# Sums of a long convolution's spectral products: the second set on VectorE instead of GpSimd

## Chip, cores and metric

One core of a Trainium2 chip runs the whole program. The metric is the device time of one execution in microseconds (us), taken as the median of several runs. The profile is one further execution, recorded by the hardware profiler.

## What is computed

A hybrid encoder layer over 512 positions and 1024 channels, batch 1, in fp32: a token mixer of three branches (long convolution, 2-D neighbourhood attention, short gated convolution), then cross-attention into 256 memory tokens, then a gated MLP. The change lies in the first branch:

```python
def long_conv(z, kf, bias):
    L = z.shape[1]
    zf32 = z.astype(jnp.float32)
    zf = jnp.fft.rfft(zf32, n=2 * L, axis=1)
    y = jnp.fft.irfft(zf * kf[None], n=2 * L, axis=1)[:, :L]
    return (y + zf32 * bias.astype(jnp.float32)).astype(z.dtype)

def hyena_mixer(u, short_w, kf, bias):
    u = dwconv3(u, short_w)
    v, x1, x2 = jnp.split(u, 3, axis=-1)
    z = x1 * long_conv(v, kf[:, 0], bias[0])
    return x2 * long_conv(z, kf[:, 1], bias[1])
```

So two convolutions of 512 channels follow each other, each gated by a projected column.

## The kernel before

Every fp32 product is made of three TensorE passes (`mm3`, lines 88 to 90) over operands that are split in a high part (`high`, L75, on ScalarE) and a low part (`low`, L78, on VectorE unless another engine is named). Weights come as 128x1024 blocks (`wr`, loaded on SyncE's queue at L110 into three buffers) and are split into `wh` and `wl`.

The long convolution runs in the loop over `parts` in `go` (two convolutions by two halves of 256 channels), four rounds that are called round 0 to 3 here. In round n the program

- makes the forward sums (`conv_forward`): PE multiplies the folded, transposed input (`sh`, `sl`) with cosine and sine waves (`wavefh`, `wavefl`, tiles `aux`), ScalarE and VectorE turn them into `fly` tiles (L523 to L529), and VectorE multiplies these by the filter's spectrum `kst` into two tiles `ab` of 128x2048 (L533 to L537): `a` and `b`, 1290 and 1291 in round 0, 1477 and 1478 in round 1;
- sums each of the two in four instructions (L543 to L546, 128x512 each, in place), the set of `a` on VectorE and the set of `b` on GpSimd;
- turns the previous round's products back (`conv_back`: PE with `waveeh`, `waveoh`; VectorE gates the result in place in `vx`, L570);
- prepares the next round's input (`conv_in`): PE transposes two `vx` tiles (L490, four instructions for each), ScalarE makes `sh`, VectorE makes `sl`;
- splits the sums for the next turn back (`conv_split`: `ych` and `ysh` on ScalarE, `ycl` and `ysl` on VectorE).

Beside these, `beside` feeds three projections per round (24 matmuls of 128x512 each, tiles `mm`) and pieces of the short convolution (`scg`, `scx`, `sct`, `yc`; L580, L323, L331, L585). A tile framework builds the program: it puts each engine's instructions in an order of its own, from the order in which the code asks for them and from its own costs, so a change of one engine moves others. On the chip each engine works through its list in that order.

GpSimd has little else here: it adds the third tap of eight projected columns (L329) and makes the low parts of some constants before, and adds attention masks (L686) later.

Of the kernel before, what the change touches and what calls it, by code (L numbers as in the profile page):

```python
# [9 lines left out]
ALU = mybir.AluOpType  # L10
# [35 lines left out]
def shaped(ap, offset, *dims):  # L46

    return bass.AP(ap.tensor, ap.offset + offset, [list(ap.ap[0])] + [list(q) for q in dims])


class Trunk:
# [444 lines left out]
    def conv_forward(self, pool, c, o, folded):  # L496


        nc, v = self.nc, self.nc.vector
        sh, sl = folded  # L500
        k = pool.tile([P, 8, 256], F32, tag="kst", bufs=1, name="kst")
        for i in range(2):
            nc.sync.dma_start(out=k[:, 4 * i : 4 * i + 4], in_=self.kd[o, c, :, 4 * i : 4 * i + 4])
        wh, wl = self.waves["f"]

        def sums(r):

            ps = self.aux_bank()
            for cs in range(2):
                w = slice((2 * r + cs) * P, (2 * r + cs + 1) * P)  # L510
                self.mm3(ps[:, cs * 256 : (cs + 1) * 256], (wh[:, w], wl[:, w]), (sh[:, r, :], sl[:, r, :]), cs == 0, cs == 1)
            return ps

        even, odd, plus = (pool.tile([P, 1024], F32, tag="fly" + q, bufs=1, name="fly") for q in "eop")
        for out, r in ((even, 0), (odd, 1)):
            low, high = out[:, 0:512], out[:, 512:1024]
            far = sums(r + 2)
            self.high(low, far[:])
            near = sums(r)
            if r:  # L520

                high = shaped(out[:], 768, [-256, 2], [1, 256])
                v.tensor_tensor(out=high, in0=near[:].rearrange("p (a b) -> p a b", a=2), in1=low.rearrange("p (a b) -> p a b", a=2),  # L523
                                op=ALU.subtract)
            else:
                v.tensor_tensor(out=high, in0=near[:], in1=low, op=ALU.subtract)
            v.tensor_tensor(out=low, in0=near[:], in1=low, op=ALU.add)
        v.tensor_tensor(out=plus[:], in0=even[:], in1=odd[:], op=ALU.add)
        v.tensor_tensor(out=even[:], in0=even[:], in1=odd[:], op=ALU.subtract)  # L529
        minus = even  # L530
        a, b = (pool.tile([P, 2048], F32, tag="ab", bufs=2, name="ab") for _ in range(2))
        kf = k[:].rearrange("p a b -> p (a b)")
        v.tensor_tensor(out=a[:, 0:1024], in0=plus[:], in1=kf[:, 0:1024], op=ALU.mult)  # L533
        v.tensor_tensor(out=a[:, 1024:2048], in0=minus[:], in1=kf[:, 1024:2048], op=ALU.mult)
        v.tensor_tensor(out=shaped(b[:], 0, [512, 2], [256, 2], [1, 256]), in0=shaped(plus[:], 0, [512, 2], [256, 2], [1, 256]),
                        in1=shaped(kf, 256, [1536, 2], [-256, 2], [1, 256]), op=ALU.mult)
        v.tensor_tensor(out=shaped(b[:], 1024, [256, 4], [1, 256]), in0=shaped(minus[:], 0, [256, 4], [1, 256]),  # L537
                        in1=shaped(kf, 1280, [-256, 4], [1, 256]), op=ALU.mult)
        for t, op, eng in ((a, ALU.add, v), (b, ALU.subtract, nc.gpsimd)):
            def part(i, step):  # L540
                return shaped(t[:], 256 * i, [256 * step, 2], [1, 256])

            eng.tensor_tensor(out=part(0, 4), in0=part(0, 4), in1=part(1, 4), op=op)  # L543
            eng.tensor_tensor(out=part(6, -4), in0=part(6, -4), in1=part(3, 4), op=op)
            eng.tensor_tensor(out=part(1, 2), in0=part(0, 6), in1=part(4, -2), op=ALU.add)
            eng.tensor_tensor(out=part(5, 2), in0=part(0, 6), in1=part(4, -2), op=ALU.subtract)  # L546
        return a, b

    def conv_split(self, pool, y):
# [798 lines left out]
```

## Time and profile before

| | |
|---|---|
| median of 3 runs | 1112.19 us (1111.86 to 1113.84) |
| the profiled execution, its own time | 1114.05 us |
| span of its instructions | 1112.3 us |
| PE busy | 1081.6 us (97% of the span) |
| VectorE (DVE) busy | 696.5 us (63%) |
| ScalarE (ACT) busy | 477.3 us (43%) |
| GpSimd (POOL) busy | 95.4 us (9%) |
| mean granted TensorE clock | 0.99 of full speed |

The span runs from the first instruction to the last, and the execution's own time holds 1.75 us more around it. An engine's busy share is a mean over stages with different limits, so a change in one stage is read from that stage. Times in the rows count from the start of the span; an instruction's line gives its start, its duration, and in brackets how long its engine sat idle before it and what ended the wait.

### The profile page before, as it was taken

How to read it: one execution, taken by the hardware profiler on the slowest of the kernel's cores; microseconds unless marked ns; L12 is line 12 of the kernel's file. 1: busy time of each engine (PE TensorE's matmuls, PEld its weight loads, DVE VectorE, ACT ScalarE, POOL GpSimd, SP SyncE). 2: the span in 40 equal slices, each digit the busy share in tenths (PEclk: the TensorE clock that was granted, in tenths of full speed). 3: DMA queues.
4: the chain of work that ended last, by engine and by line, in shares of the span. 5: the costliest groups of instructions: out<-in, count | busy, mean ns of one | idle time of the engine just before them, and what ended most of it. 6: DMA issues, size and time to landing. Idle time of an engine off the chain costs nothing.

```text
span 1112.3 us, 13562 instructions
## 1 busy us (share of the span) xinstructions
PE 1081.6 (97%) x5232; PEld 903.2 (81%) x5232; DVE 696.5 (63%) x1021; ACT 477.3 (43%) x744; POOL 95.4 (9%) x72
## 2 busy tenths in 40 slices
PE   8889989999999999999999999999999999999997
PEld 6668878887888888888789888889888888888886
DVE  6898799985656564344796546576656565642324
ACT  6553532224557453232565444454444444431221
POOL 0161242221121110000000000000000000000000
PEclk9899999999999999999999999999999999999999
DMA  6354723317423312224526421222222222222212
GB/s 218 105 190 161 246 94 107 103 58 167 125 87 100 112 57 95 95 95 160 200 76 205 156 76 57 76 95 95 95 95 95 95 95 97 102 98 101 95 57 75
DMA packets 43532, 125.48 MB, mean 113 GB/s; under 512 B 5097, under 2 KB 11561, under 8 KB 43468
## 3 DMA queue, kind: packets, MB, share of 16 engines
q1 hardware_dynamic: 43468, 124.62, 33.4%
q8 instruction: 41, 0.67, 0.2%
q14 instruction: 23, 0.19, 0.1%
HBM read 115.16 MB, written 7.34 MB: 110 GB/s over the span
## 4 chain that ended last, share of the span: by engine, by line
PE 82%; DVE 9%; DMA 3%; ACT 2%; issue 2%; POOL 1%; SPq 0%; DVEq 0%; ACTq 0%; POOLq 0%
PE mm L88 25%; PE mm L89 25%; PE mm L90 25%; DVE wl L78 2%; PE aux L725 1%; PE aux L89 1%; PE aux L90 1%; PE aux L88 1%; DMA wr<-in_w_in 1%; PE aux L714 1%; ACT wh L75 1%; PE aux L904 1%; DMA raw<-in_hy_o 1%; POOL w L398 0%; DMA wr<-in_w_out 0%
## 5 line engine op out<-in xcount | busy, mean ns | idle before, releaser
L78 DVE TENSOR_TENSOR wl<-wr,wh 128x1024 fp32r<-128x1024 f32 (+1 forms) x171 | 219.8, 1289 | 254.4 <-ACT wh L75 253.6
L75 ACT ACTIVATE wh<-wr 128x1024 fp32r<-128x1024 f32 (+1 forms) x171 | 180.1, 1054 | 308.1 <-PE mm L89 186.7
L89 PE MATMUL mm<-hl,wh 128*128 128x512 f32 (+1 forms) x448 | 167.5, 374 | 0.0
L88 PE MATMUL mm<-hh,wh 128*128 128x512 f32 (+1 forms) x448 | 167.2, 374 | 0.3 <-ACT hh L75 0.3
L90 PE MATMUL mm<-hh,wl 128*128 128x512 f32 (+1 forms) x448 | 167.4, 374 | 0.0
L88 PE MATMUL mm<-xh,wh 128*128 128x512 f32 x416 | 164.6, 396 | 0.0
L89 PE MATMUL mm<-xl,wh 128*128 128x512 f32 x416 | 163.7, 393 | 0.0
L90 PE MATMUL mm<-xh,wl 128*128 128x512 f32 x416 | 163.6, 393 | 0.0
L89 PEld LDWEIGHTS mm<-hl,wh 128*128 128x128 f32 x448 | 84.4, 188 | 15.0 <-DVE hl L78 0.2
L90 PEld LDWEIGHTS mm<-hh,wl 128*128 128x128 f32 x448 | 84.3, 188 | 15.0
L88 PEld LDWEIGHTS mm<-hh,wh 128*128 128x128 f32 x448 | 84.1, 188 | 15.2 <-ACT hh L75 0.5
L90 PEld LDWEIGHTS mm<-xh,wl 128*128 128x128 f32 x416 | 78.9, 190 | 17.1 <-issue 0.3
L88 PEld LDWEIGHTS mm<-xh,wh 128*128 128x128 f32 x416 | 79.0, 190 | 15.8
L89 PEld LDWEIGHTS mm<-xl,wh 128*128 128x128 f32 x416 | 78.9, 190 | 15.7
L88 PE MATMUL mm<-wh,act 128*128 128x512 f32 x176 | 68.5, 389 | 0.0
L89 PE MATMUL mm<-wl,act 128*128 128x512 f32 x176 | 68.5, 389 | 0.0
L90 PE MATMUL mm<-wh,act 128*128 128x512 f32 x176 | 68.3, 389 | 0.0
L88 PEld LDWEIGHTS mm<-wh,act 128*128 128x128 f32 x176 | 33.0, 188 | 7.1 <-issue 0.3
L75 ACT ACTIVATE act<-u 128x512 fp32r<-128x512 f32 x22 | 13.9, 630 | 57.8 <-DVE u L1024 57.8
L90 PEld LDWEIGHTS mm<-wh,act 128*128 128x128 f32 x176 | 33.0, 188 | 6.9
L89 PEld LDWEIGHTS mm<-wl,act 128*128 128x128 f32 x176 | 33.0, 188 | 6.8
L331 DVE SCALAR_TENSOR_TENSOR u<-mm,cols,u 128x511 f32<-128x511 f32 x44 | 33.0, 751 | 1.5
(342 smaller groups left out, 1938.4 us busy)
## 6 DMA issues: line engine op xcount, KB each, us to landing
wr<-in_w_in SPq DMA_DIRECT2D x55, 512.0 KB, 3.6
wr<-in_ffn_up SPq DMA_DIRECT2D x44, 512.0 KB, 3.5
wr<-in_ffn_down SPq DMA_DIRECT2D x22, 512.0 KB, 3.4
wr<-in_w_branch SPq DMA_DIRECT2D x12, 512.0 KB, 3.4
kd<-kt SPq DMA_DIRECT2D x16, 256.0 KB, 3.9
kst<-kd SPq DMA_DIRECT2D x8, 512.0 KB, 4.9
wr<-in_w_out SPq DMA_DIRECT2D x8, 512.0 KB, 4.3
wr<-in_xa_wk SPq DMA_DIRECT2D x8, 512.0 KB, 3.4
```

Of the source, the lines that this page charges most:

```text
L75: self.nc.scalar.activation(out=out, in_=in_, func=ACT.Copy, bias=0.0, scale=scale)
L78: (eng or self.nc.vector).tensor_tensor(out=out, in0=in_, in1=f(high), op=ALU.subtract)
L88: mm(out, ah, bh, start=first, stop=False)
L89: mm(out, ah, bl, start=False, stop=False)
L90: mm(out, al, bh, start=False, stop=last)
L331: nc.vector.scalar_tensor_tensor(out=out[:, 0 : L - 1], in0=ps[:, 1:L], scalar=self.colvec(w2), in1=out[:, 0 : L - 1], op0=ALU.mult, op1=A ...
L714: nc.tensor.transpose(tr[:, i * P : (i + 1) * P], s[:, i // 2, (i % 2) * P : (i % 2 + 1) * P], self.ident[:])
L725: self.nc.tensor.matmul(po[64 * e : 64 * e + 64, b * P : (b + 1) * P], v[b, j][:, h * 64 : (h + 1) * 64], pt[:, (2 * i + j) * P : (2 * i + ...
L904: self.nc.tensor.transpose(tr[:, k * P : (k + 1) * P], t[:, c : c + P], self.ident[:])
```

## The change

The second set of sums, those of `b`, goes to VectorE, like the first set. No instruction is added or dropped: 16 instructions of 128x512 (four in each of four rounds) leave GpSimd and join VectorE.

```diff
-        for t, op, eng in ((a, ALU.add, v), (b, ALU.subtract, nc.gpsimd)):
+        for t, op in ((a, ALU.add), (b, ALU.subtract)):
             def part(i, step):
                 return shaped(t[:], 256 * i, [256 * step, 2], [1, 256])
 
-            eng.tensor_tensor(out=part(0, 4), in0=part(0, 4), in1=part(1, 4), op=op)
-            eng.tensor_tensor(out=part(6, -4), in0=part(6, -4), in1=part(3, 4), op=op)
-            eng.tensor_tensor(out=part(1, 2), in0=part(0, 6), in1=part(4, -2), op=ALU.add)
-            eng.tensor_tensor(out=part(5, 2), in0=part(0, 6), in1=part(4, -2), op=ALU.subtract)
+            v.tensor_tensor(out=part(0, 4), in0=part(0, 4), in1=part(1, 4), op=op)
+            v.tensor_tensor(out=part(6, -4), in0=part(6, -4), in1=part(3, 4), op=op)
+            v.tensor_tensor(out=part(1, 2), in0=part(0, 6), in1=part(4, -2), op=ALU.add)
+            v.tensor_tensor(out=part(5, 2), in0=part(0, 6), in1=part(4, -2), op=ALU.subtract)
```

The framework then orders the four rounds anew. On VectorE, from round 0's first sum on, before (the numbers tell buffers apart; `vx_1335` is a projected column, `wl_1400` the low part of a weight block):

```order
L543 TENSOR_TENSOR ab_1290<-ab_1290 128x2x256
L544 TENSOR_TENSOR ab_1290<-ab_1290 128x2x256
L323 SCALAR_TENSOR_TENSOR vx_1335<-mm_1310,cols_176,vx_1335 128x511
L545 TENSOR_TENSOR ab_1290<-ab_1290 128x2x256
L546 TENSOR_TENSOR ab_1290<-ab_1290 128x2x256
L78 TENSOR_TENSOR wl_1400<-wr_1401,wh_1399 128x1024
L78 TENSOR_TENSOR sl_1375<-aux_1376,sh_1374 128x4x128
L78 TENSOR_TENSOR sl_1375<-aux_1383,sh_1374 128x4x128
```

On the same engine, from the same place on, with the change:

```order
L543 TENSOR_TENSOR ab_1290<-ab_1290 128x2x256
L544 TENSOR_TENSOR ab_1290<-ab_1290 128x2x256
L543 TENSOR_TENSOR ab_1291<-ab_1291 128x2x256
L545 TENSOR_TENSOR ab_1290<-ab_1290 128x2x256
L546 TENSOR_TENSOR ab_1290<-ab_1290 128x2x256
L544 TENSOR_TENSOR ab_1291<-ab_1291 128x2x256
L323 SCALAR_TENSOR_TENSOR vx_1335<-mm_1310,cols_176,vx_1335 128x511
L545 TENSOR_TENSOR ab_1291<-ab_1291 128x2x256
L546 TENSOR_TENSOR ab_1291<-ab_1291 128x2x256
L78 TENSOR_TENSOR sl_1375<-aux_1376,sh_1374 128x4x128
L78 TENSOR_TENSOR sl_1375<-aux_1383,sh_1374 128x4x128
```

The second set stands among the first, and the low part of the weight block has gone behind both `sl` (and behind `ycl` and `ysl`). In the same way `wl_1578`, which stood ahead of round 1's sums, now stands behind them. ScalarE's two `sh` of round 0 now stand ahead of the copy `tap` of `vx_1335`, which waits for the L323 above.

On PE, the transposes of round 1 stood in front of the projection `mm_1640`; this piece of the difference shows where they stand now:

```order
 L90 MATMUL mm_1583<-xh_427,wl_1400 128x512
-L490 MATMUL aux_1611<-ident_178,vx_455 128x128 x4
-L490 MATMUL aux_1618<-ident_178,vx_459 128x128 x4
 L88 MATMUL mm_1640<-xh_379,wh_1492 128x512
 L89 MATMUL mm_1640<-xl_380,wh_1492 128x512
 L90 MATMUL mm_1640<-xh_379,wl_1493 128x512
 L88 MATMUL mm_1640<-xh_385,wh_1492 128x512
+L490 MATMUL aux_1611<-ident_178,vx_455 128x128 x4
 L89 MATMUL mm_1640<-xl_386,wh_1492 128x512
 L90 MATMUL mm_1640<-xh_385,wl_1493 128x512
```

The first four come four matmuls later, the second four twelve; in round 2 it is one matmul and eight.

On SyncE's queue, loads of weights and of the spectrum of rounds 2 and 3, before:

```order
L110 DMA wr_1729<-in_w_in 128x1024
L110 DMA wr_1814<-in_w_in 128x1024
L503 DMA kst_1670<-kd_611 128x1024 x2
L110 DMA wr_1871<-in_w_in 128x1024
L110 DMA wr_1964<-in_w_in 128x1024
L110 DMA wr_2049<-in_w_in 128x1024
L503 DMA kst_1905<-kd_611 128x1024 x2
```

With the change:

```order
L110 DMA wr_1729<-in_w_in 128x1024
L503 DMA kst_1670<-kd_611 128x1024 x2
L110 DMA wr_1814<-in_w_in 128x1024
L110 DMA wr_1871<-in_w_in 128x1024
L110 DMA wr_1964<-in_w_in 128x1024
L503 DMA kst_1905<-kd_611 128x1024 x2
L110 DMA wr_2049<-in_w_in 128x1024
```

`wr_1814` and `wr_2049` have each gone behind the two loads of a round's spectrum. `wr_1814` takes the buffer of the block that `wl_1578` reads.

## Rows read from the trace of the kernel before

**Rows 1.** Windows: length, busy time of each engine (instructions), granted clock, DMA share, GB/s.

```profile
140.00:262.00 122.00, 115.51 (x632) 100.30 (x632) 110.67 (x119) 39.66 (x53) 30.98 (x19) 0.99 0.28 92
...
161.60:165.20 3.60, 3.60 (x17) 3.36 (x16) 3.60 (x5) 1.20 (x2) 0.00 (x0) 0.53 0.03 10
...
216.20:226.00 9.80, 8.30 (x48) 7.32 (x48) 9.24 (x13) 2.63 (x4) 0.00 (x0) 1.00 0.48 161
...
274.30:277.90 3.60, 3.60 (x10) 2.80 (x9) 3.60 (x6) 1.74 (x5) 2.00 (x2) 0.53 0.66 218
```

**Rows 2.** Timeline of PE: its waits in the four rounds, and the next one after.

```profile
160.10 0.38 PE L89 MATMUL aux<-sl,wavefh 128*128 128x256 f32 x1 [3.57 <-DVE sl L78]
...
182.90 0.75 PE L490 MATMUL aux<-ident,vx 128*128 128x128 f32 x4 [1.06 <-DVE vx L570]
...
209.32 1.34 PE L490 MATMUL aux<-ident,vx 128*128 128x128 f32 x8 [0.36 <-DVE vx L570]
...
215.76 0.39 PE L90 MATMUL mm<-xh,wl 128*128 128x512 f32 x1
215.99 0.28 PE L88 MATMUL aux<-sh,wavefh 128*128 128x256 f32 x1
217.76 0.38 PE L89 MATMUL aux<-sl,wavefh 128*128 128x256 f32 x1 [1.50 <-DVE sl L78]
...
272.84 0.36 PE L695 MATMUL aux<-kb,qa 128*128 128x256 f32 x1 [1.93 <-DMA kb<-ka]
```

**Rows 3.** Timeline of VectorE: round 0's sums, then three places of rounds 1 and 2.

```profile
150.85 0.68 DVE L543 TENSOR_TENSOR ab<-ab 128x512 f32<-128x512 f32 x1
151.46 1.78 DVE L544 TENSOR_TENSOR ab<-ab 128x512 f32<-128x512 f32 x1
153.16 0.74 DVE L323 SCALAR_TENSOR_TENSOR vx<-mm,cols,vx 128x511 f32<-128x511 f32 x1
153.82 1.11 DVE L545 TENSOR_TENSOR ab<-ab 128x512 f32<-128x512 f32 x1
154.86 1.78 DVE L546 TENSOR_TENSOR ab<-ab 128x512 f32<-128x512 f32 x1
156.56 2.29 DVE L78 TENSOR_TENSOR wl<-wr,wh 128x1024 fp32r<-128x1024 f32 x1
158.77 1.27 DVE L78 TENSOR_TENSOR sl<-aux,sh 128x512 fp32r<-128x512 f32 x2
...
176.46 0.68 DVE L543 TENSOR_TENSOR ab<-ab 128x512 f32<-128x512 f32 x1
...
184.50 1.22 DVE L78 TENSOR_TENSOR ysl<-ab,ysh 128x1024 fp32r<-128x1024 f32 x1 [1.66 <-ACT ysh L75]
...
202.88 0.68 DVE L543 TENSOR_TENSOR ab<-ab 128x512 f32<-128x512 f32 x1
```

**Rows 4.** Timeline of GpSimd in round 0.

```profile
152.65 1.73 POOL L544 TENSOR_TENSOR ab<-ab 128x512 f32<-128x512 f32 x1
154.46 1.62 POOL L545 TENSOR_TENSOR ab<-ab 128x512 f32<-128x512 f32 x1
156.04 1.72 POOL L546 TENSOR_TENSOR ab<-ab 128x512 f32<-128x512 f32 x1
```

**Rows 5.** Timelines of VectorE and GpSimd around 33.5 us, in another stage.

```profile
33.43 0.16 DVE L153 TENSOR_TENSOR rstdq<-rstdq,rstdm 128x4 f32<-128x4 f32 x1
33.62 1.18 DVE L154 TENSOR_SCALAR rstdq<-rstdq 128x4 f32<-128x4 f32 x1
...
33.49 2.52 POOL L398 TENSOR_TENSOR w<-wr 128x512 f32<-128x512 f32 x2 [33.05 <-DMA wr<-in_hy_w]
```

**Rows 6.** Timeline of ScalarE: high parts in rounds 0 and 1.

```profile
154.57 1.08 ACT L75 ACTIVATE sh<-aux 128x512 fp32r<-128x512 f32 x2
...
183.41 1.06 ACT L75 ACTIVATE ysh<-ab 128x1024 fp32r<-128x1024 f32 x1 [12.40 <-POOL ab L546]
```

**Rows 7.** DMA issues: tile, queue, count, KB each, median us from issue to landing.

```profile
wr<-in_w_in SPq DMA_DIRECT2D x55, 512.0 KB, 3.6
```

## The prediction

> **What bounds the kernel now.** I read the windows of the four rounds first. From 140 to 262 us PE works 115.51 of 122 us and VectorE 110.67 [rows 1]: PE is the bound, but VectorE is nearly as full, and the 6.49 us that PE idles there can only come from engines that feed it. PE's timeline names these waits: 3.57, 1.06, 0.36 and 1.50 us [rows 2], 6.49 together, each ended by VectorE: by `sl`, the input of the next round's sums, or by L570, the gated column that PE transposes. After the longest one PE's clock fell: from 161.6 to 165.2 us the granted clock was 0.53 of full speed, near its lower level of 1.2 GHz [rows 1], so these 3.60 us did the work of 0.53 x 3.6 = 1.9, a loss of 1.7. So 6.5 + 1.7 = 8.2 us is the most that a faster VectorE can give in this stage.
>
> Then VectorE's timeline, to see why it is late. Four instructions of one size, 128x512, all in SBUF, last 0.68, 1.78, 1.11 and 1.78 us [rows 3]. GpSimd's timeline explains the long ones: its adds end at 154.38, 156.08 and 157.76 [rows 4], and VectorE's L545, L546 and the split `wl` behind them end at 154.93, 156.64 and 158.85 [rows 3], 0.55, 0.56 and 1.09 us after these ends, which is about what each takes by itself from start to start. They had been issued earlier and were held until GpSimd's add was done. That the hold doesn't go by size is seen elsewhere: on 128x4 elements VectorE takes 0.16 us, and 1.18 us for the next one, just when GpSimd starts an add [rows 5]. Instructions that read PSUM (L323, L570, `sl`) keep their short times.
>
> **The change part by part.** *The sums.* Unheld, an add costs 0.61 us from start to start (150.85 to 151.46); held, 1.70 (154.86 to 156.56) [rows 3]. These are the two ends for each of the 32 adds that VectorE now makes. I take 0.61, since nothing of GpSimd's runs beside them but one L329 in round 0. Before, a round's set cost VectorE 156.56 - 150.85 - 0.66 (L323, 153.16 to 153.82) = 5.05 us [rows 3]; now both sets cost 8 x 0.61 = 4.88. So 16 adds come to VectorE and its list becomes 0.17 us shorter per round. GpSimd's chain ends with the set; ScalarE's `ysh`, which waited 12.40 us for it in round 1 [rows 6], follows VectorE instead.
>
> By the Trainium skill, "VectorE: DVE Perf Modes", section on the TRN2 errata, an fp32 add of N elements takes (N+151)/0.96 ns, 0.69 us for 512; that speaks against the change. If starts were so far apart, both sets would take 5.5 us, and a round would grow by 0.5 us, an estimate. The trace's duration of 0.68 agrees, but the starts lie 0.61 apart [rows 3], and these count in a full list.
>
> *Round 0.* From 150.85: eight adds 4.88, L323 0.66, so `sl` begins at 156.39 and ends 1.27 later at 157.66, because the held `wl` no longer stands ahead of it; `sh` was done at 155.65 even behind the wait that it now precedes [rows 6]. PE starts there instead of at 160.10: **2.4 us**. It then has waited 1.2 us instead of 3.57.
>
> *The clock.* After waits of 1.06 and 1.50 us PE kept full speed (1.00 around the latter), after 1.93 it fell to 0.53 for 3.6 us [rows 1, 2]. A wait of 1.2 lies with the former, so I count the whole **1.7 us**; the ends are 0 and 1.7.
>
> *Round 1.* VectorE's adds began 25.61 us after those of round 0 (176.46 - 150.85) [rows 3]. Now: less 0.17, less 1.1 (the hold on `wl`), less 1.1 (`wl_1578`, moved behind the adds): 23.2, so they start at 174.1. The first L570 is seventh and ends at 174.1 + 6 x 0.61 + 0.68 = 178.4, the second at 180.3. PE was ready for the second transposes at 181.84 (1.06 before 182.90); now 4.1 earlier, plus twelve matmuls of 0.23 (215.76 to 215.99), at 180.5: no wait. For the first it is ready eight matmuls and four transposes (0.75) before, at 177.9: 0.5 of wait [rows 2]. Of 1.06, **0.5 us** is gained.
>
> *Round 2.* Between the adds of rounds 1 and 2 lay 26.42 us (202.88 - 176.46); less 0.17 and less the idle 1.66 in front of `ysl` that `ysh` caused [rows 3], 24.6: they start at 198.7. L570 ends at 203.0; PE, 4.6 earlier than 208.96 and one matmul later, comes at 204.6. The wait of 0.36 goes. `sl` ends at 198.7 + 4.88 + two L570 1.2 + one `wl` 1.1 + 1.27 = 207.2; PE comes to it at 216.22 - 5.0 = 211.2 [rows 2]. That takes the other **1.50 us**: together **1.9**. Round 3 has no `conv_in` and PE did not wait there.
>
> *What is moved and costs nothing.* Deferred `wl` blocks are used by PE a projection or more later. `wr_1814` can only load once `wl_1578` has read its buffer, at about 181.4, and lands 3.6 later [rows 7], at 185.0; its high part then stands on ScalarE ahead of the copy of round 2's first sums, which PE ends about 185.3. Late by 0.8 at most, with VectorE busy until 186.5: nothing. Splitting the transposes costs 2 x 0.75 - 1.34 = **0.2 us** in round 2 [rows 2]. GpSimd's freed time is worth nothing. The later stages are full of PE work and start earlier; the wait of 1.93 at 272.84 follows from PE's own product and moves along.
>
> Sum: 2.4 + 1.7 + 0.5 + 1.9 - 0.2 = **6.3 us**. The profiled execution took 1114.05 us, so 1107.75 against itself; it lies 1.86 above the median of 1112.19, against which I give **1105.9 us**.
>
> **The rivals.**
>
> *A part of it only.* The clock falls after all (1.7), or GpSimd's L329, which `tap` now releases at about 156, holds round 0's last add for 1.1 [rows 3]. Against the first: the waits above. Against the second: the add starts at about 155.7. Also, a weight load of some 2 us more would use up the 1.6 us between L570 and PE in round 2. Time: 1107.6 with the one, 1108.7 with both.
>
> *No change.* VectorE is full, and work put on it costs what it takes: 16 x 0.61 = 9.8 us. If the first set kept its 5.05 us, the adds would cost 3 x 2.4 = 7.3 more up to round 2's `sl`. What goes away before that place is the idle of 1.66 twice (a like one follows in round 2), the hold of 1.1, and `ycl`, `ysl` and one `wl` (3.4 together) that are now behind `sl`: 7.8. PE then starts at 217.76 about as before: 1112. The three matching ends [rows 3, 4] speak against it. The Trainium skill, "Perfetto Trace Analysis", section "Optimizing Scalar/DVE Operations", says that with a full VectorE moving work to GpSimd may make sense, adding that the two share a read port; by its first half the change goes the wrong way.
>
> *Slower.* The long adds are long by themselves: L544 writes with a negative step, and L546 takes 1.78 as well. Then the second set costs 5.05 too. Up to 217.76 three rounds add 15.2, less the 7.8 above: PE starts 7.4 later, 1119.6. It decides from about 0.96 us per add, (3 x 5.05 + 7.8) / 24. For it: four durations that return in each round. Against: L545 reads and steps as L546 does and takes 1.11; and a hold of 1.0 on 128x4 [rows 3, 5].
>
> **How the numbers follow.** Forecast 0.56, a part 0.27, no change 0.09, slower 0.08. The low end: without the waits of 0.5 and the 0.2 and with the fall of clock at 274.3 [rows 1] gone too, 2.4 less: 1103.5. The high end takes in both parts of the first rival and some 1.5 of further waits: 1110.2. No change and slower, 0.17, are left out. About 0.2%, 2.2 us, is what a measurement can tell: faster by more holds the forecast and nearly all of the first rival, 0.81; within it, 0.11; slower, 0.08.
>
> **What would show it.** VectorE's 32 adds at 0.68 us each; no hold on the `wl` of round 0; `sl` of round 0 done near 157.7; PE's waits of 140 to 262 us down from 6.5 to some 2; clock 1.00 from 157 to 175; the first L695 wait some 6 us earlier with the same 1.9. Adds of 1.1 or 1.7 us without GpSimd beside them would make the reason wrong; new waits of PE for `wh`, `wl` or L570 above 2 us, the size.

## The result

With the change the kernel takes **1104.49 us** (median of 6 runs, 1101.96 to 1106.84), before it took 1111.34 in the same comparison (6 runs, 1108.24 to 1113.84). The ratio is 0.9935, with a 95% interval of 0.9919 to 0.9952: 0.65% faster, 7.2 us by the ratio. Forecast were 1105.9 us, 6.3 less than before. The profiled execution after took 1105.53 us, its span is 1103.8 (before 1112.3).

The page of the changed kernel, its span and busy times:

```profile
span 1103.8 us, 13552 instructions
...
PE 1079.7 (98%) x5232; PEld 902.4 (82%) x5232; DVE 693.4 (63%) x1037; ACT 477.1 (43%) x744; POOL 68.2 (6%) x56
```

VectorE got 16 instructions more and is 3.1 us less busy (696.5 before). Windows of the same kernel, columns as in [rows 1]:

```profile
140.00:262.00 122.00, 120.69 (x668) 105.03 (x667) 112.52 (x139) 44.58 (x61) 7.63 (x6) 1.00 0.33 105
157.00:175.00 18.00, 16.69 (x108) 15.05 (x107) 18.00 (x22) 5.68 (x7) 1.29 (x1) 1.00 0.19 68
...
264.00:284.00 20.00, 18.88 (x89) 15.29 (x88) 10.29 (x17) 12.36 (x20) 3.96 (x4) 1.00 0.54 165
```

PE idles 1.31 us of these 122, where it idled 6.49 [rows 1], and the clock stays at full speed behind that wait, and from 264 to 284 us as well, behind the wait at L695. VectorE's timeline after, to be held against [rows 3]:

```profile
152.64 0.69 DVE L543 TENSOR_TENSOR ab<-ab 128x512 f32<-128x512 f32 x1
153.24 0.68 DVE L544 TENSOR_TENSOR ab<-ab 128x512 f32<-128x512 f32 x1
...
155.65 0.69 DVE L544 TENSOR_TENSOR ab<-ab 128x512 f32<-128x512 f32 x1
156.25 0.74 DVE L323 SCALAR_TENSOR_TENSOR vx<-mm,cols,vx 128x511 f32<-128x511 f32 x1
...
157.51 0.69 DVE L546 TENSOR_TENSOR ab<-ab 128x512 f32<-128x512 f32 x1
158.11 1.28 DVE L78 TENSOR_TENSOR sl<-aux,sh 128x512 fp32r<-128x512 f32 x2
...
175.57 0.68 DVE L543 TENSOR_TENSOR ab<-ab 128x512 f32<-128x512 f32 x1
...
185.05 1.22 DVE L78 TENSOR_TENSOR ysl<-ab,ysh 128x1024 fp32r<-128x1024 f32 x1
```

All 32 sums last 0.68 or 0.69 us and start 0.60 apart, L544 and L546 as well, which had taken 1.78 (with L323 or L570 between two sums, their starts lie 1.20 to 1.26 apart). `ysl` no longer waits (1.66 before). PE's timeline at the places of [rows 2]:

```profile
159.45 0.39 PE L89 MATMUL aux<-sl,wavefh 128*128 128x256 f32 x1 [1.31 <-DVE sl L78]
...
179.92 0.75 PE L490 MATMUL aux<-ident,vx 128*128 128x128 f32 x4
...
205.40 0.63 PE L490 MATMUL aux<-ident,vx 128*128 128x128 f32 x4
...
207.26 0.63 PE L490 MATMUL aux<-ident,vx 128*128 128x128 f32 x4
...
211.64 0.28 PE L88 MATMUL aux<-sh,wavefh 128*128 128x256 f32 x1
211.75 0.28 PE L89 MATMUL aux<-sl,wavefh 128*128 128x256 f32 x1
...
265.60 0.36 PE L695 MATMUL aux<-kb,qa 128*128 128x256 f32 x1 [0.80 <-DMA kb<-ka]
```

The transposes of rounds 1 and 2 and round 2's `sl` have no wait any more; the waits of 1.06, 0.36 and 1.50 us are gone, that of 3.57 is 1.31.

**Where the 8.5 us between the two spans come from.** Three stretches, each bounded by the same instruction in both traces. Up to round 0's first sum the program is the same, and this execution was 1.79 us later (152.64 against 150.85): a difference between executions. From there to round 3's last L570 it took 103.28 us before (150.85 to 254.13) and 95.46 now (152.64 to 248.10): 7.8 won. The remaining 2.5 us were won behind the rounds. 7.8 + 2.5 - 1.8 = 8.5.

### The profile page after: what moved, and what is told of

Same layout as the page of the kernel before. It is cut to its first block, busy times and chain, and to the rows that moved or that the text cites. A ratio compares the mean times of both kernels' runs of the same rounds, so it can differ in the third digit from the quotient of the medians.

```text
span 1103.8 us, 13552 instructions
## 1 busy us (share of the span) xinstructions
PE 1079.7 (98%) x5232; PEld 902.4 (82%) x5232; DVE 693.4 (63%) x1037; ACT 477.1 (43%) x744; POOL 68.2 (6%) x56
## 3 DMA queue, kind: packets, MB, share of 16 engines
q1 hardware_dynamic: 43468, 124.62, 33.5%
## 4 chain that ended last, share of the span: by engine, by line
PE 86%; DVE 5%; DMA 4%; ACT 2%; issue 1%; SPq 1%; POOL 1%; DVEq 0%; ACTq 0%; POOLq 0%
PE mm L89 26%; PE mm L88 26%; PE mm L90 26%; PE aux L89 2%; PE aux L90 2%; PE aux L88 2%; PE aux L725 1%; DMA wr<-in_w_out 1%; DVE wl L78 1%; PE aux L714 1%; DMA raw<-in_hy_o 1%; PE aux L904 1%; POOL w L398 1%; ACT wh L75 0%; DMA v<-vd 0%
```

## The experiments

The theory: a GpSimd instruction that reads SBUF holds VectorE's instructions with two inputs in SBUF (they are issued, and end only after it has ended); without it the same sums cost 0.6 us. The first rival: the long sums are long by themselves. The second: what helped is the new order (`sl` ahead of the weight block, `sh` ahead of `ych`), which the change brought along. All ratios are to the kernel before.

**The order alone.** GpSimd keeps the second set; `sl` is issued ahead of the weight blocks' low parts, and `ych` and `ysh` behind `sh`. The edit shifts line numbers by 3 to 6 (L570 is L576 here, L546 is L551).

```diff
...
+    behind = None
...
-        (eng or self.nc.vector).tensor_tensor(out=out, in0=in_, in1=f(high), op=ALU.subtract)
+        with self.tc.issue_after(self.behind) if self.behind is not None and eng is None else ExitStack():
+            self.last = (eng or self.nc.vector).tensor_tensor(out=out, in0=in_, in1=f(high), op=ALU.subtract)
...
+            self.behind = None
             self.split(sh[:, :, cs], sl[:, :, cs], t3)
+            self.behind, self.copied = self.last.ins, self.copy.ins
...
-            self.split(h[:], lo[:], shaped(t[:], 256, [512, 4], [1, 256]))
+            with self.tc.issue_after(self.copied):
+                self.split(h[:], lo[:], shaped(t[:], 256, [512, 4], [1, 256]))
```

> The order alone: GpSimd keeps the second set, but VectorE's `sl` and ScalarE's `sh` are put ahead of the weight splits and of `ych`/`ysh`, as the change has them. Theory (the holds on VectorE are the main price, the order follows): PE starts round 1's sums near 158 instead of 160.1 and its clock stays at 1.00, but the adds of `a` are still held (1.78, 1.11, 1.78 us) and VectorE's list is as long as before, so PE waits more for L570 in round 1 (some 4 us instead of 1.06); in all a gain of 2 to 3.5 us, about 1108 to 1109.5. Rival (the order is what gained): PE's waits between 140 and 262 us fall to some 1.5 us as with the change, about 1104.5.

Measured: 1110.58 us (12 runs) against 1112.54 (23 runs of before), ratio 0.9984, 0.9971 to 0.9997: some 1.8 us. PE's waits from 135 to 270 us (engine, tile and line that waited, what for: total, times, longest), in this kernel:

```profile
PE aux L493 <- DVE vx L576: 4.2, 3, 2.6
PE aux L92 <- DVE sl L81: 1.5, 1, 1.5
```

and its VectorE in round 0:

```profile
154.13 1.79 DVE L549 TENSOR_TENSOR ab<-ab 128x512 f32<-128x512 f32 x1
...
157.54 1.78 DVE L551 TENSOR_TENSOR ab<-ab 128x512 f32<-128x512 f32 x1
159.24 1.28 DVE L81 TENSOR_TENSOR sl<-aux,sh 128x512 fp32r<-128x512 f32 x2
```

The order shortens the wait for `sl` to 1.54 us, but the sums are held as before, and VectorE's late L570 makes PE wait 4.2 us in rounds 1 and 2. By the medians the order gives about a quarter of the gain (1.8 of 7.2 us), a little less than I had expected; in the traces it gives 2.8 of the 7.8 us of the rounds (153.53 to 254.02, 100.49 against 103.28). The rival, by which it gives all, falls; a part of the gain is the order's.

**The same sums on VectorE, with others on GpSimd beside them.** The changed kernel, and four GpSimd adds per round on a tile that nothing reads any more:

```diff
+        for _ in range(4):
+            nc.gpsimd.tensor_tensor(out=plus[:, 0:512], in0=plus[:, 0:512], in1=plus[:, 512:1024], op=ALU.add)
```

> The change, with four GpSimd adds of 128x512 per round beside it that nothing waits for (they read and write a dead tile, from the end of L535 on). Theory (an instruction of VectorE with two SBUF inputs waits while a GpSimd add runs): three or four of VectorE's adds per round last 1.1 to 1.8 us again, VectorE's list grows by some 3 to 4.4 us per round, less than 4 us of that is hidden, so 1108 to 1113. Rival (order, or that nothing waits for GpSimd any more): VectorE's adds stay at 0.68 us and the time at 1104.5, within 1 us.

Measured: 1119.93 us (6 runs), ratio 1.0067, 1.0049 to 1.0084: slower than the kernel before. GpSimd's adds in round 0 (four in one row, 7.27 us together):

```profile
149.99 7.27 POOL L548 TENSOR_TENSOR fly<-fly 128x512 f32<-128x512 f32 x4 [7.45 <-DVE ab L535]
```

VectorE in the same place:

```profile
150.96 1.78 DVE L543 TENSOR_TENSOR ab<-ab 128x512 f32<-128x512 f32 x1
152.67 1.77 DVE L544 TENSOR_TENSOR ab<-ab 128x512 f32<-128x512 f32 x1
154.37 1.77 DVE L543 TENSOR_TENSOR ab<-ab 128x512 f32<-128x512 f32 x1
156.06 1.74 DVE L545 TENSOR_TENSOR ab<-ab 128x512 f32<-128x512 f32 x1
157.73 0.68 DVE L546 TENSOR_TENSOR ab<-ab 128x512 f32<-128x512 f32 x1
```

GpSimd's four adds end at 157.26. While they run, each of VectorE's sums takes 1.74 to 1.78 us; the first one after them takes 0.68. The order doesn't decide it: on VectorE, ScalarE, PE and SyncE's queue the trace has, by line and tile, the same order as the changed kernel's, here and in the next run. Nor does the instruction decide it: L543, which was always short, is long here, and L546, which was long [rows 3], is short. The fourth sum ends at 157.80, 0.54 after GpSimd's last, as in the trace of before (0.55). What PE waited for from 135 to 270 us:

```profile
PE aux L490 <- DVE vx L572: 6.5, 2, 3.6
PE aux L89 <- DVE sl L78: 6.2, 1, 6.2
```

The direction was as expected, the size not: 1108 to 1113 us had left room for some 4 to 8 us, and it cost some 15 more than the change without them. VectorE is 15.9 us busier (709.3 against 693.4), that is 16 holds of 1.0; and behind such waits the mean clock of 140 to 262 us was 0.94, which I had not counted.

**Four GpSimd instructions that only write.** The same kernel with memsets in place of the adds, in the same order on every other engine:

```diff
+        for _ in range(4):
+            nc.gpsimd.memset(plus[:, 0:512], 0.0)
```

> As the run with the GpSimd adds beside, instruction for instruction in the same order, but GpSimd writes zeros into the same places (it reads nothing). By the Trainium skill, SBUF — State Buffer, section Who interferes with whom, such an instruction holds nobody up. Theory: adds of VectorE stay at 0.68 us, the time at 1104.5 within 1.5 us. Rival (any GpSimd instruction in flight holds VectorE): as the run with the adds, 1108 to 1113.

Measured: 1103.12 us (6 runs), ratio 0.9916, 0.99 to 0.9933, no difference from the change itself. GpSimd in round 0:

```profile
148.07 2.27 POOL L548 MEMSET fly<- 128x512 f32 x4 [5.81 <-DVE ab L535]
```

VectorE beside it:

```profile
149.06 0.68 DVE L543 TENSOR_TENSOR ab<-ab 128x512 f32<-128x512 f32 x1
149.67 0.69 DVE L544 TENSOR_TENSOR ab<-ab 128x512 f32<-128x512 f32 x1
```

The memsets run until 150.34, beside the first two sums, and hold neither. So GpSimd's being at work is not the cause; what the adds do and the memsets don't is read SBUF (a GpSimd instruction with a single input was not run). The Trainium skill, "SBUF — State Buffer", section "Who interferes with whom", states this: a VectorE instruction with two SBUF inputs contends with a GpSimd instruction that reads SBUF, and not with one that only writes it. These two runs agree: 1.74 to 1.78 us with the adds, 0.68 and 0.69 with the memsets.

**The change in round 0 only.**

```diff
-        for t, op in ((a, ALU.add), (b, ALU.subtract)):
+        for t, op, eng in ((a, ALU.add, v), (b, ALU.subtract, v if (c, o) == (0, 0) else nc.gpsimd)):
```

> The change in round 0 alone; rounds 1 to 3 as before. Theory: PE starts round 1's sums near 157.7 and the clock does not fall (4.1 us gained there), but VectorE's list of rounds 1 and 2 is as long as before, so part of this comes back as a longer wait for L570 in round 1 (some 2.5 to 3 us instead of 1.06): in all 2 to 2.5 us, about 1109. Rival (the fall of the clock is what counts): 4 us, about 1107.3.

Measured: 1111.75 us (12 runs), ratio 0.9994, 0.9983 to 1.0004: no difference that can be told. PE's waits from 135 to 270 us:

```profile
PE aux L490 <- DVE vx L570: 3.9, 2, 2.6
PE aux L89 <- DVE sl L78: 2.1, 2, 1.4
```

Windows of the same kernel:

```profile
209.50:213.10 3.60, 3.60 (x11) 2.82 (x10) 2.62 (x3) 3.35 (x6) 0.00 (x0) 0.54 0.00 0
...
272.00:283.00 11.00, 10.38 (x49) 8.34 (x48) 7.97 (x14) 7.16 (x14) 3.84 (x4) 1.00 0.62 180
```

Round 0's wait for `sl` is 1.44 instead of 3.57, and then it is lost again: VectorE's list in rounds 1 and 2 is as long as before, PE comes earlier and waits 3.9 us for L570, and the fall of the clock now follows the 2.6 of it. My expectation of 2 to 2.5 us missed: it took round 0's gain for kept.

**The change in rounds 1 to 3 only**: the same line with `(c, o) != (0, 0)`.

> The change in rounds 1 to 3 only; round 0's second set stays on GpSimd. If the wait of 3.57 us and the fall of the clock behind it belong to round 0's held instructions, they stay (5.3 us together), and only the 2.9 us of the later waits can go: 1107.5 to 1110 us. The first round alone gave less than 1 us, because its gain was lost again in rounds 1 and 2 (waits of 1.28, 0.62 and 2.60). If the two parts simply add up to the whole, this one gives some 6 us: about 1105. I hold the former, with the rest of the whole's gain given only by both together.

Measured: 1107.01 us (5 runs) against 1112.78 (11), ratio 0.9955, 0.994 to 0.9969: 5.0 us. PE's waits from 135 to 270 us:

```profile
PE aux L89 <- DVE sl L78: 3.2, 1, 3.2
PE aux L695 <- DMA kb<-ka: 0.5, 1, 0.5
```

As expected, round 0's long wait stays, and the clock is 0.54 behind it (from 161.5 to 165.2 us). But the gain is 5 us and not 2.9. The trace says where: from round 0's first sum to the last L570 it is 4.0 us shorter (151.01 to 250.28, 99.27), and 2.0 come behind the rounds, where I had expected nothing (more on this below). Within the rounds the two parts give 0.8 (102.52 against 103.28) and 4.0, together 3 us less than the 7.8 of the whole. That the first round's gain is kept only if the later lists are short too is what I take from this. The medians (0.7 and 5.0 against 7.2) point the same way, but their intervals do not settle it.

**GpSimd's work of the filter stage on VectorE too.** From 60 to 90 us the changed kernel has the same signs: VectorE full, GpSimd at work beside it, PE waiting for VectorE. Ten instructions were moved: the low parts of cosine and sine, and the filter weights' sums and low parts.

```diff
-                self.split(h[:, c], lo[:, c], raw[:], nc.gpsimd)
+                self.split(h[:, c], lo[:, c], raw[:])
...
-            nc.gpsimd.tensor_tensor(out=w3[:, i * CH : (i + 1) * CH], in0=raw[:, 0:CH], in1=raw[:, CH:], op=op)
-        self.split(w3a[:], w3b[:], w3[:], nc.gpsimd)
+            nc.vector.tensor_tensor(out=w3[:, i * CH : (i + 1) * CH], in0=raw[:, 0:CH], in1=raw[:, CH:], op=op)
+        self.split(w3a[:], w3b[:], w3[:])
```

> The change, and beside it the filter stage's work of GpSimd (the low parts of cosine and sine, the sums of the filter's weights and their low parts: 10 instructions, 22.7 us of GpSimd) on VectorE too. It tests whether the mechanism carries over to another stage in which VectorE is full (29.0 of 30 us from 60 to 90 us) and PE waits for it (3.6 us for hf, some 1.8 of clock). If each of these ten holds a VectorE instruction for 1.1 us or more (11 to 15 us in all) and costs VectorE only 0.6 to 1.2 by itself (7.2 in all), VectorE is 4 to 7 us earlier there and PE gets back 1 to 4: 1100.5 to 1103.5 us. If work on a full VectorE costs what it takes there: 1106 to 1111.

Measured: **1093.63 us** (4 runs, 1090.55 to 1095.02), ratio 0.9828, 0.981 to 0.9847: by the ratios 12 us below the change, beyond all that I expected, and the fastest kernel of this study. The window in the changed kernel,

```profile
60.00:90.00 30.00, 24.63 (x100) 19.31 (x99) 29.00 (x35) 15.08 (x23) 18.83 (x8) 0.94 0.45 151
```

and in this one:

```profile
60.00:90.00 30.00, 30.00 (x137) 24.99 (x136) 29.45 (x46) 16.61 (x26) 2.97 (x2) 1.00 0.58 195
```

VectorE does 46 instructions there in place of 35, PE 137 in place of 100; 37 matmuls of 0.23 us are 8.5 us. VectorE's timeline there, in the changed kernel:

```profile
66.47 4.52 DVE L78 TENSOR_TENSOR wl<-wr,wh 128x1024 fp32r<-128x1024 f32 x2
...
80.30 2.44 DVE L78 TENSOR_TENSOR la<-hf,ha 128x512 fp32r<-128x512 f32 x1 [1.00 <-ACT ha L75]
```

and with the ten instructions moved (the first row is from the stage of [rows 5]):

```profile
34.13 0.17 DVE L154 TENSOR_SCALAR rstdq<-rstdq 128x4 f32<-128x4 f32 x1
...
60.43 2.35 DVE L78 TENSOR_TENSOR wl<-wr,wh 128x1024 fp32r<-128x1024 f32 x2
62.70 1.29 DVE L78 TENSOR_TENSOR cosl<-raw,cosh 128x512 fp32r<-128x512 f32 x2
```

A split of 128x512 took 2.44 us there, not 0.68: GpSimd's low part `w3b` ran from 79.83 to 82.19, and this one ended 0.55 later. Unheld, the four halves of cosine and sine cost VectorE 2.4 us, where GpSimd took 9.8 for them. Even the tiny L154, 1.18 us in [rows 5], is 0.17 once GpSimd doesn't work beside it. This L154 has one input in SBUF (the other operands are constants), so the theory's "two inputs" is too narrow; which other instructions with one input are held, no run sorts out. My estimate counted one hold of 1.1 per GpSimd instruction, but seven of them take 17.7 us in this window (18.83 less 1.09 for one L329), 2.5 each, and a hold lasts until its GpSimd instruction has ended.

The rest of the 12 us was won before 60 us, where PE does 16 matmuls more (216 against 200). Most of them fall between 40 and 50 us, in the changed kernel

```profile
40.00:50.00 10.00, 7.51 (x26) 6.08 (x27) 10.00 (x18) 3.91 (x7) 0.00 (x0) 0.83 0.22 79
```

and in this one:

```profile
40.00:50.00 10.00, 10.00 (x38) 8.09 (x37) 9.41 (x18) 6.27 (x10) 0.00 (x0) 0.83 0.17 68
```

The clock is the same there. VectorE reaches L274, behind the first three of the ten instructions, at 36.44 us instead of 40.35. From 10 to 20 us the clock was 1.00 here and 0.73 in the changed kernel, for which I have no cause, but little hangs on it: with the taps moved as well (the second run below) it was 0.83 there, and PE had done its 216 by 60 us too.

**The third tap of the columns on VectorE too**, from PSUM, alone and with the filter stage's work:

```diff
-        self.conv3(t[:], got[:], [HYW + tap * 12 + blk for tap in range(3)], blk not in (0, 1, 4, 5))
+        self.conv3(t[:], got[:], [HYW + tap * 12 + blk for tap in range(3)], False)
```

> The change, and beside it the third tap of all columns on VectorE, from PSUM (0.66 us each, as the other columns have it), in place of a ScalarE copy and a GpSimd add (L329, 8 times, 1.35 us). Eight holds of up to 1.1 go, eight instructions of 0.66 come: VectorE gains at most 3.5 us, spread over 110 us in which PE hardly waits. By the holds: 1103 to 1105.5 us, within what a measurement tells. If work on VectorE costs what it takes: up to 1108.

> The two further moves together, so that GpSimd has no two-input work before the attention masks but the low parts of two waves. By the holds 1100 to 1103.5 us, the sum of the two alone; by VectorE's work 1107 to 1113.

Measured: 1102.54 us (6 runs), ratio 0.9915, 0.9899 to 0.9932, and 1095.36 (5 runs), ratio 0.9847, 0.9829 to 0.9865. Neither can be told from the same kernel without this move (0.9935 and 0.9828): where PE hardly waits, this move gives nothing that can be measured. VectorE isn't less busy by it either (694.7 us in the first of the two, against 693.4). The second lies below what I had expected, for the filter stage's reason.

## Why the prediction was right

**The sums, as argued.** I took 0.61 us each, both sets 4.88; they took 4.81 (152.64 to 158.11, less 0.66 for L323). "No change" and "slower" rested on sums that cost what they add or are long by themselves; the two runs with GpSimd's adds and memsets beside them exclude both. Of the page named with "no change" (the Trainium skill, "Perfetto Trace Analysis", section "Optimizing Scalar/DVE Operations") its second half holds here, that moving work between the two may not help because they share a read port: the 16 sums moved back made VectorE 3.1 us less busy.

**Round 0, to the tenth.** I had `sl` let PE go 6.81 us behind the first sum (150.85 to 157.66), with 1.2 us of wait left; it was 6.81 (152.64 to 159.45) and 1.31: 2.4 us, as the sum has it.

**The clock.** No fall behind the 1.31, so the whole 1.7 came, as counted. The reason was weaker than it looked; see below.

**Rounds 1 and 2: 0.7 us too little.** The step that put 0.5 us of new wait before round 1's first transposes failed: the L570 for them was done at 179.86, 27.2 us behind round 0's first sum (I had 27.5), and PE came at 179.92, 27.3 behind (I had 27.0). Two errors of 0.2 to 0.3 made a wait out of none. Nor did the split transposes cost 0.2: in round 2 two rows of 0.63 stand where one of 1.34 stood. With both back the sum would be 7.0. That is what the waits (6.49 - 1.31 = 5.2) and the clock (1.7) give; the other 0.9 of the 7.8 I had not traced. About half of it is that a wait costs PE more than its idle time: from 215.99 to 217.76 [rows 2] is 1.77, where the same two starts now lie 0.11 apart (211.64 to 211.75), so 1.66 went with an idle of 1.50. Three waits went whole; at 0.16 each that is 0.5.

**Behind the rounds: the step that failed.** I wrote that the wait of 1.93 at L695 "follows from PE's own product and moves along". It did not: 0.80 now, and there is no fall of the clock behind it (1.00 from 264 to 284 us, where [rows 1] have 0.53 from 274.3 to 277.9). That is 1.1 + 1.7 = 2.8 at most, of which 2.5 are seen. The profile gives the source of the 1.1: the transfer that the wait is for, from issue to landing, before

```profile
kb<-ka SPq DMA_DIRECT2D x4, 128.0 KB, 4.8
```

and after:

```profile
kb<-ka SPq DMA_DIRECT2D x4, 128.0 KB, 3.7
```

What made the transfer faster was not tested and stays open, but the traces rule out two causes. It is not the changed order of SyncE's queue: from 215.44 us on before, and from 212.79 after, the same loads are issued in the same order. And it doesn't need a shorter list of VectorE: with the order alone, where the sums are held, the wait is short, and with the change in round 0 only it is as long as before:

```profile
271.44 0.36 PE L701 MATMUL aux<-kb,qa 128*128 128x256 f32 x1 [0.64 <-DMA kb<-ka]
```

```profile
271.35 0.36 PE L695 MATMUL aux<-kb,qa 128*128 128x256 f32 x1 [1.93 <-DMA kb<-ka]
```

With GpSimd's adds beside, in the slowest kernel of all, it is 0.86. Behind the last L570 the kernel with the order alone takes 855.28 us (1109.3 - 254.02), the kernel before 858.17, the changed one 855.70. So the 2.5 us are not shown to come from the sums. The execution that was profiled before lies 1.86 above its median, and a part of the 2.5 may be its own. The fall at 274.3 was in my low end and not in the forecast.

So the profiles have 10.3 us won in place of 6.3, less the 1.8 by which this execution came late to the rounds; the medians, 6.9 by difference and 7.2 by the ratio, lie between. That the forecast of 6.3 came so near them is in part luck: the rounds gave 1.5 more than the sum has, and the stretches outside them, which the sum doesn't have, moved by 2.5 one way and 1.8 the other.

**A part of it only** did not happen. L329 ran at 157.85 for 1.29 us when only the last sum was left, and held nothing. `wr_1814` landed late as reckoned: its high part began at 186.41, and one instruction of VectorE moved by 0.1 us.

## What to carry to other kernels

Where VectorE is full and GpSimd adds or subtracts in SBUF beside it, read VectorE's durations of one form with and without GpSimd at work: if they differ, GpSimd's share is paid for by VectorE, and taking it back can shorten VectorE's list. Do it for a whole stretch between PE's waits, since a gain in one round is lost to the next round's longer list. Then look for the same sign in other stages; here the filter stage gave more than the change itself.

## What was not expected of the hardware

The length of PE's last wait did not decide whether the clock fell from full speed to near its lower level of 1.2 GHz. It fell to 0.54 after 2.60 us (the change in round 0 only, 209.5 to 213.1 us), and stayed at 1.00 after 2.61 us (the order alone, L493 at 184.20, the window from 183 to 193). After 1.93 us in front of L695 it fell in the kernel before [rows 1] and stayed in the kernel with round 0 only (the window from 272 above). So my comparison of waits in the prediction gave the right answer for a reason that does not hold.

A GpSimd memset of 128x512 takes 0.57 us (2.27 / 4), and an add of that size 1.8 beside VectorE's sums (7.27 / 4).
